# Low parts of the weights last in each split product; the convolution of x ahead of the attention's gate in the first layer

## The chip, the cores and the metric

The kernel runs on one core of one Trainium2 chip. The metric is device time in microseconds (us), from one launch that holds the whole computation. A core has five engines that each work through a queue of their own in order: TensorE (PE, with its weight loads, PEld), VectorE (DVE), ScalarE (ACT), GpSimd (POOL) and SyncE (SP, which here only issues transfers). They wait for one another through semaphores; transfers (DMA) run beside them.

## The reference, cut to what matters

Two layers over 512 tokens of x and 256 tokens of a context, with 1024 channels. Each layer has a trunk (normalization, one input projection, three token mixers that gates merge, an output projection) and a feed-forward part of 16,384 one-neuron experts, of which each of 8 heads picks 16 for a token.

```python
for l in range(2):
    p = modulate(rms_norm(h)) @ w_in[l]                  # 1024 -> q, k, v, pool, conv (3 x), gates (3 x)
    attn = attn_out_norm(diff_attn(q, [k, kc], [v, vc])) # kc, vc: from the context's projection
    pool = pool_branch(p_pool, pool_w[l])
    conv = (b_gate * depthwise_conv(c_gate * p_conv)) @ conv_out_w[l]
    g = sigmoid(p_gates)
    h = h + mod * ((g0 * attn + g1 * pool + g2 * conv) @ w_out[l])
    # experts, in chunks of 128 tokens
    q = (xn2 @ w_q).reshape(T, 8, 2, 128)
    s1, i1 = top_k(q[:, :, 0] @ keys1, 16); s2, i2 = top_k(q[:, :, 1] @ keys2, 16)
    top_s, pos = top_k(s1[:, None] + s2, 16); eidx = (i1 * 128 + i2)[pos]
    hid = gelu(xn2 . u_emb[eidx]);  w = softmax(top_s) * hid
    h = h + mod * sum(w * v_emb[eidx])
    # the context hc goes the same way in the first layer (in the last only its k and v are made)
```

All is in float32.

## The kernel before, in words

**Split products.** Every large product is made of operands that are split into a high part (rounded to TensorE's format) and a low part (the rest): `split` (line 92) copies the high part on ScalarE and subtracts it on VectorE, for weights as for activations. `mm3` (lines 96 to 100) then issues three matmuls for each of the 8 slices of the contracted dimension, all into one bank of the accumulation memory: high by high, high by low, low by high. In `proj_t`, `hidden` and `values` the weight is the left operand, so the third matmul of every slice reads the low part of the weight: `wlo` in a projection, `ul` in the experts' first product, `vl` in their second.

**Weights.** `load_w` (line 136) fetches a projection's weight as two halves of four slices on SyncE's queue into `wraw` (three buffers) and splits each into `whi` and `wlo` (three buffers each). `proj_t` (line 153) makes a group of 24 matmuls for a 128-row block of the result.

**Mixers.** `mixers` (line 980) goes through a string of letters: p pooling, c convolution, g attention's gate with the norm of its heads, k the convolution's gates made ahead, o merge and output projection. Over x in the first layer the string is "gco" with three banks for the results (line 972). Just before stand the norm and the top-16 picks of the context's feed-forward part (`ctx_ffn`).

**Experts.** The context (256 tokens) in the first layer and the first 128 tokens of x in the second are done row by row: `gathered` (line 848) has GpSimd fetch for every one of the 128 picks of 128 tokens a row of `peer_u` or `peer_v` by index into a ring of three `row` buffers (line 855); VectorE multiplies and sums it (lines 868 and 878). There are 768 fetches. Their priority is 40000 behind their place in the program, so they are spread under later work. All other tokens (512 of x in the first layer, 384 in the second) go through all experts densely: `gates` (line 750 on) builds with one-hots `gA`, `gE`, `gB` on VectorE and small matmuls `gps` a table of gate weights `G`; `hidden` (line 767) makes gelu(u y) in tiles of 128 experts, `uh` and `ul` in two buffers each; `weigh` (line 796) multiplies it with `G` and splits the product into `wh` and `wl`; `values` (line 820) multiplies with the experts' second weights, blocks of 8 tiles, `vh` and `vl`, in four banks `dps`. In the second layer 20 of 32 chunks of hidden products are stored first; for the other 12, `experts` (line 1123) goes through hidden and values in turn, with EC + 2 = 4 buffers for `vh` and `vl`.

**What sets the order.** The code gives every instruction a priority by its place in the program, shifted in places by `prio`; a scheduler with a simulated time line then writes out one fixed order for every engine, in which buffers and data allow it. On the chip each engine works strictly in that order.

**Stages in the trace (us).** To 360 modulation, norm and q, k, v of the first layer; to 850 attention, the context's mixers and pooling; to 1360 the context's keys and the mixers over x; 1380 to 2290 keys, gates and hidden products; to 3000 values; to 3790 the second layer's trunk; to 4400 its keys, gates and stored hidden products; 4415 to 4730 hidden and values in turn; to the end the rest of the values. Fetches of rows run from 997 to 2874 and from 3800 on.

## Time and profile before

| | |
|---|---|
| median of 3 runs | 5121.54 us (5118.99 to 5127.41) |
| profiled execution | 5126.48 us |
| its span, from first to last instruction | 5124.7 us |
| mean granted clock of TensorE | 0.975 |
| TensorE busy | 4846.5 us, 95% |
| its weight loads busy | 4187.1 us, 82% |
| VectorE busy | 3946.3 us, 77% |
| ScalarE busy | 1984.5 us, 39% |
| GpSimd busy | 1199.9 us, 23% |

The busy time of TensorE counts the whole of each matmul, with ends that are modelled, so a busy TensorE can still be slower than at its pace. The list of waits puts each idle time of an engine down to the work that ended it, as engine, tile, line <- engine, tile, line. A window gives the busy time of each engine within a stretch, and the clock granted there as a share of full speed.

### The profile page before, as it was taken

Reading aid. Unit: us, or ns where it says so; the run is one execution under the profiler, and the core shown is the slowest. Engines: PE = TensorE matmul, PEld = TensorE weight load, DVE = VectorE, ACT = ScalarE, POOL = GpSimd, SP = SyncE. Lnnn points to the kernel's source line nnn. Section 1 sums busy time; section 2 is a strip of 40 time slices with the busy share of each in tenths; the row PEclk is TensorE's granted clock in tenths of the full one; section 3 lists DMA queues with packets and bytes.
Section 4 is the critical chain, followed back from the end, with each engine's and each line's share of the span. In section 5 each row is a group of like instructions: output and inputs, shape, how many; then the busy total and the mean of one; then the engine's idle time right before and its main releaser. Section 6 shows DMA issues by size and latency. Waiting matters only on the chain.

```text
span 5124.7 us, 74008 instructions
## 1 busy us (share of the span) xinstructions
PE 4846.5 (95%) x27373; PEld 4187.1 (82%) x27373; DVE 3946.3 (77%) x7996; ACT 1984.5 (39%) x2970; POOL 1199.9 (23%) x1060
## 2 busy tenths in 40 slices
PE   8999999798799999989999999999999999899999
PEld 5689787576588788768888879888679889899999
DVE  5468785977799998568888766777459999787885
ACT  4346665222233344323222334555334344332333
POOL 0012000144433343243334100100000433244320
PEclk9999999899899999999999999999899999999999
DMA  8668554488888888999999734543355888988995
GB/s 308 239 201 237 179 169 129 145 271 276 281 302 270 297 300 323 323 315 320 342 335 337 261 114 161 175 135 118 120 169 173 282 297 329 319 313 292 335 330 177
DMA packets 509419, 1280.77 MB, mean 250 GB/s; under 512 B 42880, under 2 KB 225024, under 8 KB 500736
## 3 DMA queue, kind: packets, MB, share of 16 engines
q1 hardware_dynamic: 302816, 669.35, 38.7%
q0 software_dynamic: 132352, 449.90, 26.1%
q10 hardware_dynamic: 73888, 156.79, 8.2%
q8 instruction: 215, 3.52, 0.3%
q14 instruction: 148, 1.21, 0.1%
HBM read 1098.13 MB, written 177.73 MB: 249 GB/s over the span
## 4 chain that ended last, share of the span: by engine, by line
PE 47%; DMA 14%; issue 11%; DVE 9%; POOL 3%; ACT 1%; POOLq 0%; DVEq 0%; ACTq 0%; SPq 0%
DMA row<-peer_v,ix 8%; PE dps L100 6%; PE dps L99 6%; PE dps L98 6%; DMA row<-peer_u,ix 5%; PE mm L98 4%; PE mm L100 4%; PE mm L99 4%; PE hid L100 4%; PE hid L98 4%; PE hid L99 3%; POOL row L855 3%; DVE gacc L878 2%; PE gps L760 1%; PE qk L100 1%
## 5 line engine op out<-in xcount | busy, mean ns | idle before, releaser
L100 PE MATMUL hid<-yh,ul 128*128 128x512 f32 (+1 forms) x2048 | 760.8, 373 | 55.3 <-DVE ul L94 54.9
L855 POOL DMA_INDIRECT row<-peer_v,ix x384 | 586.7, 1528 | 876.9 <-DVE gacc L878 537.4
L98 PE MATMUL hid<-yh,uh 128*128 128x512 f32 (+1 forms) x2048 | 758.3, 371 | 21.0 <-ACT yh L286 13.1
L855 POOL DMA_INDIRECT row<-peer_u,ix x384 | 503.5, 1311 | 1113.7 <-DVE row L868 614.3
L99 PE MATMUL hid<-yl,uh 128*128 128x512 f32 (+1 forms) x2048 | 755.9, 369 | 3.6 <-DVE yl L287 3.6
L100 PE MATMUL dps<-wh,vl 128*128 128x512 f32 (+1 forms) x2048 | 740.9, 364 | 11.8 <-DVE vl L94 11.8
L99 PE MATMUL dps<-wl,vh 128*128 128x512 f32 (+1 forms) x2048 | 741.1, 364 | 7.0 <-DVE wl L94 7.0
L98 PE MATMUL dps<-wh,vh 128*128 128x512 f32 (+1 forms) x2048 | 735.3, 364 | 8.9 <-ACT vh L93 8.9
L98 PE MATMUL mm<-hi,whi 128*128 128x512 f32 (+1 forms) x1856 | 665.5, 359 | 19.6 <-ACT rg L481 6.0
L100 PE MATMUL mm<-hi,wlo 128*128 128x512 f32 (+1 forms) x1856 | 658.6, 357 | 25.3 <-DVE wlo L94 25.0
L99 PE MATMUL mm<-lo,whi 128*128 128x512 f32 (+1 forms) x1856 | 659.8, 356 | 1.7 <-DVE lo L94 1.7
L878 DVE SCALAR_TENSOR_TENSOR gacc<-row,gw,gacc 128x1024 f32<-128x1024 f32 x381 | 488.2, 1281 | 166.9 <-DMA row<-peer_v,ix 165.4
L868 DVE SCALAR_TENSOR_TENSOR row<-row,gx 128x1024 f32<-128x1024 f32 x384 | 466.9, 1222 | 168.5 <-DMA row<-peer_u,ix 167.9
L94 DVE TENSOR_TENSOR wlo<-wraw,whi 128x1024 fp32r<-128x1024 f32 (+1 forms) x356 | 428.1, 1204 | 178.5 <-ACT whi L93 175.7
L93 ACT ACTIVATE uh<-uraw 128x1024 fp32r<-128x1024 f32 x256 | 271.3, 1060 | 689.5 <-PE hid L99 657.4
L93 ACT ACTIVATE whi<-wraw 128x1024 fp32r<-128x1024 f32 (+1 forms) x356 | 369.9, 1043 | 385.3 <-PE mm L99 270.1
L93 ACT ACTIVATE vh<-vraw 128x1024 fp32r<-128x1024 f32 x256 | 270.1, 1057 | 633.6 <-PE dps L99 387.9
L100 PEld LDWEIGHTS hid<-yh,ul 128*128 128x128 f32 x2048 | 391.2, 191 | 107.4 <-DVE ul L94 69.3
L98 PEld LDWEIGHTS hid<-yh,uh 128*128 128x128 f32 x2048 | 392.1, 192 | 63.6 <-ACT yh L286 14.7
L100 PEld LDWEIGHTS dps<-wh,vl 128*128 128x128 f32 x2048 | 386.3, 189 | 53.2 <-DVE vl L94 12.7
L99 PEld LDWEIGHTS hid<-yl,uh 128*128 128x128 f32 x2048 | 391.4, 191 | 44.7 <-DVE yl L287 5.0
L98 PEld LDWEIGHTS dps<-wh,vh 128*128 128x128 f32 x2048 | 386.6, 189 | 49.9 <-ACT vh L93 9.7
(337 smaller groups left out, 9481.1 us busy)
## 6 DMA issues: line engine op xcount, KB each, us to landing
uraw<-uT SPq DMA_DIRECT2D x256, 512.0 KB
vraw<-v SPq DMA_DIRECT2D x256, 512.0 KB
wraw<-w_in SPq DMA_DIRECT2D x216, 512.0 KB
gd<-gst ACTq DMA_DIRECT2D x28, 2048.0 KB
mw<-w_mod SPq DMA_DIRECT2D x96, 512.0 KB
wraw<-wq SPq DMA_DIRECT2D x80, 512.0 KB
hidd<-ge ACTq DMA_DIRECT2D x128, 256.0 KB
G<-gd SPq DMA_DIRECT2D x32, 1024.0 KB
```

Of the source, the lines that this page charges most:

```text
L93: self.nc.scalar.activation(hi, src, AF.Copy)
L94: self.nc.vector.tensor_tensor(lo, src, hi.bitcast(F32), op=OP.subtract)
L98: mm(ps, lh, rh, start=start, stop=False)
L99: mm(ps, lh, rl, start=False, stop=False)
L100: mm(ps, ll, rh, start=False, stop=stop)
L760: nc.tensor.matmul(ps[:, t], A[:, a_, :, t_], B[x][:, a_, :, t_], start=x == 0, stop=x == 1)
L855: nc.gpsimd.indirect_dma_start(out=r, out_offset=None, in_=a[t], in_offset=bass.IndirectOffsetOnAxis(ap=idx[:, s:s + 1], axis=0))
L868: nc.vector.scalar_tensor_tensor(out=r, in0=r, scalar=1.0, in1=x, op0=OP.mult, op1=OP.mult, accum_out=hid[:, k:k + 1])
L878: nc.vector.scalar_tensor_tensor(acc, r, w[:, k:k + 1], acc, op0=OP.mult, op1=OP.add)
```

## The change

`mm3` takes all slices of a group at once. It issues two matmuls for each slice first, and only then the third of every slice. With `late` 0 these last ones are those that read the low part of the left operand, with 1 those of the right operand; each call picks the one that is the weight. The number of matmuls stays the same. `uh` and `ul` get three buffers for two. In the turns of the second layer `vh` and `vl` get three for four. In the mixers over x in the first layer the convolution comes ahead of the attention's gate ("cgo"), the results have six banks for three, and the second half of every weight gets buffers from a pool of its own, `wmore`, three each beside the three there were. The numbers of the lines behind shift by 1 to 5.

```diff
-    def mm3(self, ps, lh, ll, rh, rl, start, stop):
+    def mm3(self, ps, terms, late, start=True, stop=True):
         mm = self.nc.tensor.matmul
-        mm(ps, lh, rh, start=start, stop=False)
-        mm(ps, lh, rl, start=False, stop=False)
-        mm(ps, ll, rh, start=False, stop=stop)
+        for i, (lh, ll, rh, rl) in enumerate(terms):
+            mm(ps, lh, rh, start=start and i == 0, stop=False)
+            mm(ps, *((lh, rl), (ll, rh))[late], start=False, stop=False)
+        for i, (lh, ll, rh, rl) in enumerate(terms):
+            mm(ps, *((ll, rh), (lh, rl))[late], start=False, stop=stop and i == len(terms) - 1)
...
     def load_w(self, src, kts, cols):
...
-            h = self.wpool.tile([P, step, cols], F32R, tag="whi", name="whi", bufs=self.wbufs)
-            lw = self.wpool.tile([P, step, cols], F32R, tag="wlo", name="wlo", bufs=self.wbufs)
+            pool, n = (self.wmore, 3) if k0 and self.wmore else (self.wpool, self.wbufs)
+            h = pool.tile([P, step, cols], F32R, tag="whi", name="whi", bufs=n)
+            lw = pool.tile([P, step, cols], F32R, tag="wlo", name="wlo", bufs=n)
...
     def proj_t(self, pp, w, streams, kts=KT, tag="mm"):
...
-            for k in range(kts):
-                self.mm3(ps, w[0][k], w[1][k], s.h[:, k], s.l[:, k], k == 0, k == kts - 1)
+            self.mm3(ps, [(w[0][k], w[1][k], s.h[:, k], s.l[:, k]) for k in range(kts)], 0)
...
     def hidden(self, l, y, up, uq, cs, ahead, keep=False):
...
-                    uh = up.tile([P, KT, P], F32R, name="uh", bufs=2)
-                    ul = up.tile([P, KT, P], F32R, name="ul", bufs=2)
+                    uh = up.tile([P, KT, P], F32R, name="uh", bufs=3)
+                    ul = up.tile([P, KT, P], F32R, name="ul", bufs=3)
...
-                for k in range(KT):
-                    self.mm3(hid, uh[:, k], ul[:, k], y.h[:, k], y.l[:, k], k == 0, k == KT - 1)
+                self.mm3(hid, [(uh[:, k], ul[:, k], y.h[:, k], y.l[:, k]) for k in range(KT)], 0)
...
     def values(self, l, n, cs, W, pools, vq, acc, first, last=None):
...
-                for e in range(4 * EC):
-                    self.mm3(ps, V[e][0][:, db * P:(db + 1) * P], V[e][1][:, db * P:(db + 1) * P], W[0][e], W[1][e],
-                             e == 0, e == 4 * EC - 1)
+                b = slice(db * P, (db + 1) * P)
+                self.mm3(ps, [(V[e][0][:, b], V[e][1][:, b], W[0][e], W[1][e]) for e in range(4 * EC)], 0)
...
-        self.EC, self.stored = 2, 20
+        self.EC, self.stored, self.wmore = 2, 20, None
...
                 with ExitStack() as e2:
-                    hm = self.mixers(l, X, self.pool(e2, f"fl{l}", 3, PSUM), xp, "gco")
+                    self.wmore = self.pool(e2, f"wx{l}")
+                    hm = self.mixers(l, X, self.pool(e2, f"fl{l}", 6, PSUM), xp, "cgo")
+                self.wmore = None
...
-                        self.values(l, n, cs, self.weigh(l, n, va, cs, had), lambda dq: (vb, 3, vb, EC + 2), vq, acc, c == S + EC)
+                        self.values(l, n, cs, self.weigh(l, n, va, cs, had), lambda dq: (vb, 3, vb, EC + 1), vq, acc, c == S + EC)
```

On TensorE, inside one tile of hidden products in the second layer (`hid` is the result, `yh` and `yl` the parts of the tokens, `uh` and `ul` of the weight), before, two slices and the start of the third:

```order
L98 MATMUL hid<-yh,uh 128x384
L99 MATMUL hid<-yl,uh 128x384
L100 MATMUL hid<-yh,ul 128x384
L98 MATMUL hid<-yh,uh 128x384
L99 MATMUL hid<-yl,uh 128x384
L100 MATMUL hid<-yh,ul 128x384
L98 MATMUL hid<-yh,uh 128x384
```

and now, the last three slices of a tile and the beginning of the next tile:

```order
L101 MATMUL hid<-yh,uh 128x384
L102 MATMUL hid<-yl,uh 128x384
L101 MATMUL hid<-yh,uh 128x384
L102 MATMUL hid<-yl,uh 128x384
L101 MATMUL hid<-yh,uh 128x384
L102 MATMUL hid<-yl,uh 128x384
L104 MATMUL hid<-yh,ul 128x384 x8
L101 MATMUL hid<-yh,uh 128x384
```

The eight matmuls that read `ul`, one in each slice before, stand together behind the sixteen that read `uh`.

On TensorE, around the norm of the context ahead of its keys in the first layer (`nps` is the sum of squares, `ntr` the transposes; `po` is the context attention's or x's attention output, `mm` a projection), before:

```order
L100 MATMUL mm<-hi,wlo 128x512
L275 MATMUL nps<-nsq,ones 128x256 x2
L293 MATMUL ntr<-ident,nfull 128x128 x10
L98 MATMUL mm<-hi,whi 128x512
L99 MATMUL mm<-lo,whi 128x512
```

and now:

```order
L456 MATMUL tr_6337<-ident,at 128x128 x4
L101 MATMUL po<-th,hv_6152 128x512
L102 MATMUL po<-th,hv_6153 128x512
L104 MATMUL po<-tl,hv_6152 128x512
L280 MATMUL nps<-nsq,ones 128x256 x8
L298 MATMUL ntr<-ident,nfull 128x128 x16
L101 MATMUL mm<-hi,whi 128x256
L102 MATMUL mm<-lo,whi 128x256
```

The projections of the attention's gate (`mm` with 512 columns) that stood between the parts of the norm have left; the norm's matmuls stand together between the last attention product and the first key projection (256 columns).

On VectorE, at the end of the second layer's gates (`gA`, `gE`, `gB` one-hots of the gates; `gacc` and `row,ghid` fetched rows; `ul` the splits of hidden weights), before:

```order
L878 SCALAR_TENSOR_TENSOR gacc<-row,gw,gacc 128x1024
L94 TENSOR_TENSOR ul<-uraw,uh 128x1024
L750 TENSOR_TENSOR gA<-iota_38404,sl_35870 128x1024
L752 TENSOR_TENSOR gB_40098<-gE,sl_35872 128x1024
L753 TENSOR_TENSOR gB_40099<-gE,sl_35873 128x1024
L878 SCALAR_TENSOR_TENSOR gacc<-row,gw,gacc 128x1024
L94 TENSOR_TENSOR ul<-uraw,uh 128x1024
L878 SCALAR_TENSOR_TENSOR gacc<-row,gw,gacc 128x1024 x3
L94 TENSOR_TENSOR ul<-uraw,uh 128x1024
L868 SCALAR_TENSOR_TENSOR row,ghid<-row,gx 128x1024 x2
L94 TENSOR_TENSOR ul<-uraw,uh 128x1024 x2
```

and now:

```order
L879 SCALAR_TENSOR_TENSOR gacc<-row,gw,gacc 128x1024
L754 TENSOR_TENSOR gE<-iota_38408,sl_35875 128x1024
L755 TENSOR_TENSOR gB_40074<-gE,sl_35876 128x1024
L756 TENSOR_TENSOR gB_40075<-gE,sl_35877 128x1024
L753 TENSOR_TENSOR gA<-iota_38408,sl_35874 128x1024
L755 TENSOR_TENSOR gB_40102<-gE,sl_35876 128x1024
L756 TENSOR_TENSOR gB_40103<-gE,sl_35877 128x1024
L879 SCALAR_TENSOR_TENSOR gacc<-row,gw,gacc 128x1024
L869 SCALAR_TENSOR_TENSOR row,ghid<-row,gx 128x1024 x6
L811 TENSOR_TENSOR ge<-ge,G 128x384 x4
L94 TENSOR_TENSOR wl<-ge,wh 128x384 x3
```

The splits `ul` that stood between and behind the last gate instructions have moved ahead of them; behind the last gate come six fetched rows and then at once the product of hidden and gate (`ge<-ge,G`, line 809 before, 811 now).

## Rows read from the trace of the kernel before

**Rows 1.** The page's busy table: engine, busy us, share of the span, instructions.

```profile
PE 4846.5 (95%) x27373; PEld 4187.1 (82%) x27373; DVE 3946.3 (77%) x7996; ACT 1984.5 (39%) x2970; POOL 1199.9 (23%) x1060
```

**Rows 2.** TensorE's waits, whole span: us in total, times, longest us.

```profile
PE hid L100 <- DVE ul L94: 54.9, 33, 5.8
PE mm L100 <- DVE wlo L94: 28.9, 16, 4.2
...
PE dps L100 <- DVE vl L94: 11.8, 2, 11.0
...
PE dps L98 <- ACT vh L93: 8.9, 2, 7.1
```

**Rows 3.** Windows: stretch, length, busy us by engine, granted clock, DMA share, GB/s.

```profile
1060.00:1340.00 280.00, 242.72 (x996) 191.77 (x994) 203.78 (x252) 67.17 (x83) 121.25 (x107) 0.96 0.82 274
1380.00:2290.00 910.00, 880.67 (x4974) 736.30 (x4973) 770.77 (x1704) 322.75 (x484) 330.35 (x231) 0.99 0.87 303
2434.00:2562.00 128.00, 128.00 (x567) 106.01 (x566) 110.61 (x148) 36.23 (x46) 46.33 (x36) 1.00 0.97 341
3960.00:4388.00 428.00, 402.86 (x2787) 384.39 (x2786) 396.38 (x828) 175.28 (x283) 159.27 (x99) 0.98 0.83 300
4415.00:4730.00 315.00, 295.37 (x1647) 291.70 (x1648) 248.77 (x336) 104.24 (x149) 125.58 (x91) 0.97 0.88 304
```

**Rows 4.** Waits of TensorE, then VectorE, in 1060 to 1340.

```profile
PE mm L100 <- DVE wlo L94: 21.9, 12, 4.2
...
DVE row L868 <- DMA row<-peer_u,ix: 30.2, 17, 3.9
```

**Rows 5.** Lines in 1060 to 1340: count, busy us, mean ns, idle before.

```profile
L878 DVE SCALAR_TENSOR_TENSOR gacc<-row,gw,gacc 128x1024 f32<-128x1024 f32 x49 | 62.9, 1283 | 38.4 <-DMA row<-peer_v,ix 38.2
...
L868 DVE SCALAR_TENSOR_TENSOR row<-row,gx 128x1024 f32<-128x1024 f32 x48 | 58.3, 1222 | 30.2 <-DMA row<-peer_u,ix 30.2
...
L94 DVE TENSOR_TENSOR wlo<-wraw,whi 128x1024 fp32r<-128x1024 f32 x41 | 50.0, 1219 | 0.0
...
L585 DVE SCALAR_TENSOR_TENSOR y<-z,cols,y 128x512 f32<-128x512 f32 x6 | 4.5, 753 | 0.2
...
L600 ACT ACT_TABLE_LOAD x2 | 2.6, 1283 | 0.0
```

**Rows 6.** Timeline of TensorE from 848 to 890: start, us, instruction.

```profile
848.61 0.39 PE L98 MATMUL mm<-hi,whi 128*128 128x512 f32 x1
...
888.77 0.39 PE L98 MATMUL mm<-hi,whi 128*128 128x256 f32 x1
```

**Rows 7.** TensorE's waits in 1380-2290, 2290-3000, 3790-4415 and (three) 4415-4730.

```profile
PE hid L100 <- DVE ul L94: 16.8, 12, 4.0
...
PE dps L100 <- DVE vl L94: 11.0, 1, 11.0
...
PE hid L100 <- DVE ul L94: 24.4, 13, 5.8
...
PE hid L100 <- DVE ul L94: 13.7, 8, 5.0
PE dps L98 <- ACT vh L93: 7.1, 1, 7.1
PE dps L100 <- DVE vl L94: 0.7, 1, 0.7
```

**Rows 8.** VectorE's waits in 3960 to 4388.

```profile
DVE row L868 <- DMA row<-peer_u,ix: 14.3, 8, 4.6
DVE gacc L878 <- DMA row<-peer_v,ix: 11.6, 7, 5.5
DVE ul L94 <- ACT uh L93: 2.4, 4, 0.9
```

**Rows 9.** Timeline of ScalarE's queue, then VectorE, in 4380 to 4420.

```profile
4389.27 0.33 ACTq L763 DMA_DIRECT2D gd<-gst  x1
...
4415.14 1.96 DVE L809 TENSOR_TENSOR ge<-ge,G 128x384 f32<-128x384 f32 x4
```

More of the change, by code (lines that the diff above doesn't have):

```diff
@@ L315, in qkv @@
                             for t in range(2):
-                                for k in range(KT):
-                                    xh, xl = s.sub(k, 2 * u + t)
-                                    self.mm3(ps[:, t], xh, xl, w[0][k], w[1][k], k == 0, k == KT - 1)
+                                self.mm3(ps[:, t], [(*s.sub(k, 2 * u + t), w[0][k], w[1][k]) for k in range(KT)], 1)
                             if kind == "v":
@@ L456, in head @@
             self.split(th, tl, tr)
-            self.mm3(po, v[0][:, kt], v[1][:, kt], th, tl, kt == 0, kt == nk - 1)
+            self.mm3(po, [(v[0][:, kt], v[1][:, kt], th, tl)], 1, kt == 0, kt == nk - 1)
         ot = ap_.tile([P, nq * P], F32, tag="ot", name="ot", bufs=2)
@@ L777, in hidden @@
                     nc.sync.dma_start(raw.rearrange("p k e -> p (k e)"), a["uT"][l, 4 * c + e])
-                    uh = up.tile([P, KT, P], F32R, name="uh", bufs=2)
-                    ul = up.tile([P, KT, P], F32R, name="ul", bufs=2)
+                    uh = up.tile([P, KT, P], F32R, name="uh", bufs=3)
+                    ul = up.tile([P, KT, P], F32R, name="ul", bufs=3)
                     self.split(uh, ul, raw)
                 hid = uq.tile([P, y.n], F32, name="hid", bufs=3)
-                for k in range(KT):
-                    self.mm3(hid, uh[:, k], ul[:, k], y.h[:, k], y.l[:, k], k == 0, k == KT - 1)
+                self.mm3(hid, [(uh[:, k], ul[:, k], y.h[:, k], y.l[:, k]) for k in range(KT)], 0)
                 with self.prio(-ahead):
```

## The prediction, made before the changed kernel had run

> **What bounds the kernel now.** I read the page's busy table first. TensorE (PE) is busy for 4846.5 of 5124.7 us, which looks like no room; its weight loads and VectorE (DVE) stand well below [rows 1]. A busy PE is not a PE at its pace, so I took the pace from a stretch without holes: 567 matmuls of 512 columns in 128.0 us at clock 1.00, 0.226 us each [rows 3]. Next the list of PE's waits: the four that the change aims at are weights' low parts made by DVE, `ul` 54.9, `wlo` 28.9, `vl` 11.8 us, and a smaller one for a high part, `vh` 8.9 [rows 2]. Together 104.5 us, 2% of the time.
>
> Then I asked which engine keeps PE waiting in each stretch. In the first layer's mixers over x, 996 matmuls would take 225 us of the 280 there [rows 3]: 55 us are lost, and 21.9 of them is the wait for `wlo` [rows 4]. DVE is busy for 203.8 us of the same 280, and sits another 68.4 us (38.2 + 30.2) in front of a gathered row that has not landed [rows 3, 5]. It works in the order written, so 272 of 280 us are spoken for: splits stand behind late rows. 97 rows (49 + 48) pass there [rows 5], one every 2.89 us, though DVE needs only 1.25 for one; the ring of three `row` buffers (line 855) goes round no faster.
>
> **What the change does not touch.** PE carries 28,735 rows in its queue before and after; no matmul is added. ScalarE gets 11 more table loads of 1.283 us [rows 5], 14 us in all on an engine at 39%; I price them at nothing, and at 14 us if all stood on the path.
>
> **Term 1: first layer, mixers over x, -22 us.** In the old order 96 matmuls of the gates (21.7 us at 0.226) stand between and around the context's norm, from 848.61 until the first key projection at 888.77 [rows 6]; in the new one the norm's matmuls stand alone and nothing covers its chain. The 40.2 us shrink to no less than 18.5; I take 22, so the keys start 18 us earlier, and the 96 matmuls are issued later instead. Behind the keys the convolution runs where the old order had the gate's norm; its first three weights are split before DVE's long top-16 work, six groups of 24, 33 us of matmuls. But six more `wlo` and about ten smaller instructions of the convolution now stand ahead of the first fetched row on DVE: 6 x 1.219 plus 10 x 0.75 [rows 5] is 14.8 us, less some 5 for the eleven short instructions of the norm that leave this place (bounded by 0 and 11 x 0.75). So fetching starts 18 - 10 = 8 us earlier. From there DVE's order has 112 fetches before the last tile of the output projection, where it had 117: 5 x 2.89 is 14 us. 8 + 14 = 22. If fetches set the end, the extra `wlo` buffers and six banks give no more. Ends: +5 if the bare norm and the gate's norm chain, now among fetches at 2.89 us each, cost what is saved; -45 if PE alone sets the end (the 55 lost less 10).
>
> **Term 2: first layer, hidden products, -18.** PE waits 16.8 us there for `ul` [rows 7], and the clock is at 0.99 over 910 us [rows 3], some 9 us of work lost. Low parts are now needed 16 matmuls (3.6 us) later and three buffers let a split start a whole tile (24 matmuls, 5.4 us) earlier; the longest of all such waits was 5.8 [rows 2]. I take 14 of the waits and 4 of the clock. Ends: -26 and -4 (DVE, busy 770.8 of 910 [rows 3], hands the delay on).
>
> **Term 3: first values, -7.** The one wait of 11.0 us for `vl` [rows 7] falls behind 32 matmuls with high parts (four groups of eight), 7.2 us. Ends -9 and 0.
>
> **Term 4: handover of the products' right sides, 0.** `wh` of a block is now read until the last eight matmuls of its last group, so the next block's splits have 9 to 16 matmuls where they had over 20. Four groups are interleaved there, eight matmuls per part (1.8 us), against some 0.75 us of DVE (128x512 [rows 5]). About 30 handovers at up to 0.4 us: 0 to +12.
>
> **Term 5: second layer until the first values, 0.** PE waits 24.4 us for `ul` [rows 7], and I give back none of it. DVE is busy 396.4 of 428 us and waits 25.9 (14.3 + 11.6) for rows [rows 3, 8]: it is the bound. The new order runs PE's hidden tiles ahead of the gates, until their buffers are full, and leaves the last five gate rounds alone on DVE; the last gate has 226 splits `ul` in front of it instead of 219 and 303 of the fetches' second kind instead of 300. 7 x 1.219 plus 3 x 1.283 [rows 5] is 12.4 us more DVE work, against 2.4 us of DVE's waits for `uh` [rows 8], and I take 10 of the row waits, as fetches now stand evenly, one per four gate instructions. From the last gates' write to the first product of hidden and gate lie 25.9 us (4389.27 to 4415.14) [rows 9], which the old order fills with four hidden tiles and the new one leaves empty; those tiles were done before. What remains behind that point is the same, so the end moves only as the last gate moves. Ends -12 and +12.
>
> By occupancy the row says DVE 396.4 against weight loads 384.4 of 428. The Trainium skill (Perfetto Trace Analysis, Identifying the Most-Contended Engine) says to improve the engine with the highest occupancy, judging TensorE by its weight loads. This change takes no instruction off DVE; by that rule term 5 is 0, as I have it, and term 2, where DVE also leads (770.8 to 736.3), would fall to -4 and the sum to -47.
>
> **Term 6: second layer, rest, -10.** `ul` 13.7 and `vh` 7.1 [rows 7] go, 20.8. In the loop that mixes hidden and values, `vh` and `vl` have three buffers instead of four: the second tile of each of 24 quarter blocks waits until the tile before is read, 24 matmuls (4.3 us at 295.37 / 1647 = 0.179 [rows 3]) for two splits (2 x 1.22 = 2.4 [rows 5]). I charge 0.5 us for each of 22, 11. Ends -22 and +20.
>
> **Term 7: elsewhere, -4** (28.9 - 21.9 = 7.0 of `wlo` [rows 2, 4]); ends -7 and 0.
>
> Sum: -22 - 18 - 7 + 0 + 0 - 10 - 4 = -61. The profiled execution took 5126.5 us (span 5124.7 and 1.8 around it), so 5065.5; the median run, 5121.5, lies 5 lower, so 5060.5. I predict 5060.
>
> **Rivals.** *All of it comes out*: the four waits and nothing given back, 5121.5 - 104.5 = 5017. For it: the waits are short (33 of `ul`, the longest 5.8) and a whole tile of lead covers them; against it: 272 of 280 us of DVE in term 1, and term 5.
> *Handed on*: DVE's queue, fetches and splits in one order, is the bound almost everywhere, and PE waits at another place. Then only term 3 is left: 5114. For it: the late rows [rows 4, 8]; against: in 1380 to 2290 DVE has 139 us free.
> *Slower*: three buffers in the mixed loop. Place: second `vl` of each quarter block, behind late rows on DVE. At 4 us per block, about one late row (the row waits of the first layer ran to 3.9 [rows 4]), it costs 24 x 4 = 96 instead of 11, and the sum becomes +24: 5146. It decides from 61 / 24 = 2.5 us per block above my 0.5. Against it: PE's waits for `vl` there are 0.7 us now, in all [rows 7].
>
> **Chances.** Forecast 0.62, all of it 0.15, handed on 0.13, slower 0.10. A difference under 0.2% (10 us, below 5111 or above 5132) can't be told from none. Half of "handed on" lies beyond it: faster 0.62 + 0.15 + 0.06 = 0.83, same 0.07, slower 0.10. The forecast's own range is 5030 to 5090 (terms 1 and 6 at half of their ends). For 8 in 10 I leave out the slow rival and the upper part of "handed on", and keep "all of it" but for its lowest part: 5012 to 5112.
>
> **What would show it.** In the changed profile: PE's waits for `ul` and `vl` under 10 us in all (terms 2, 3, 6); rows still at about 2.9 us apart in the first layer's mixers, with its last output tile about 22 us earlier (term 1); an idle PE for 25 to 45 us ahead of the second layer's first values, with the last gate at most 12 us later counted from the stage's start (term 5); waits for `vl` below 0.5 us per quarter block (term 6). Rows that come faster than 2.9 us apart, or PE idle in the mixed loop, would make it wrong.

## The result, and the profile after

The change made the kernel slower: 5190.14 us (median of 4 runs, 5187.74 to 5197.82) against 5122.34 before; ratio 1.0134, 95% interval [1.0117, 1.0152]. The forecast was 5060 with a range of 5012 to 5112. The profiled execution took 5197.82 us, its span 5196.1, 71.4 more than before.

The busy table hardly differs from [rows 1]; ScalarE has 11 instructions more:

```profile
PE 4866.2 (94%) x27373; PEld 4202.6 (81%) x27373; DVE 3936.6 (76%) x7996; ACT 2018.2 (39%) x2981; POOL 1234.9 (24%) x1060
```

TensorE's waits over the whole span (us, times, longest), which answer to [rows 2]:

```profile
PE dps L102 <- DVE wl L94: 29.3, 20, 4.2
PE dps L101 <- ACT vh L93: 28.7, 4, 24.8
PE nps L280 <- ACT nsq L279: 24.6, 9, 12.1
PE dps L101 <- ACT wh L93: 23.2, 10, 14.3
PE hrb L505 <- ACT hrh L93: 22.1, 2, 17.4
PE sc L437 <- ACT p L444: 18.5, 16, 2.3
PE hss L495 <- ACT osq L494: 15.6, 2, 14.0
...
PE dps L104 <- DVE vl L94: 13.7, 5, 7.3
PE gps L763 <- ACT gst L765: 12.4, 8, 4.7
...
PE mm L104 <- DVE wlo L94: 3.0, 1, 3.0
```

Four of these waits before, which [rows 2] leave out:

```profile
PE hrb L502 <- ACT hrh L93: 13.9, 2, 9.2
...
PE nps L275 <- ACT nsq L274: 9.5, 6, 5.2
...
PE hss L492 <- ACT osq L491: 7.0, 2, 6.8
PE dps L99 <- DVE wl L94: 7.0, 5, 3.4
```

`ul` is gone from the list and `wlo` has shrunk from 28.9 to 3.0. Which edit took them away the list does not say; the experiments do, and for `wlo` it is not the late order. In their place stand `wl`, `vh` and `wh`, the operands of the second expert product, `p`, the attention's exponentials, and ScalarE's steps in the norms (`nsq` for the norm of all channels, `osq` and `hrh` for the norm of attention's heads). The list got no shorter, so I went to a table by stage: the time of one first or last matmul of a tile in TensorE's timeline, in each profiled execution. (`rsc` are the scores of the context's keys, `hid` and `dps` the two expert products; 0 and 1 are the layers.)

| us | before | after | difference | gained or lost in the stage |
|---|---|---|---|---|
| first `rsc` (end of the attention stage and the context's norm) | 900.6 | 933.1 | +32.5 | +32.5 |
| first `hid`, 0 (end of the mixers over x) | 1361.8 | 1390.1 | +28.3 | -4.2 |
| first `dps`, 0 (end of hidden) | 2286.2 | 2310.7 | +24.5 | -3.8 |
| last `dps`, 0 (end of values) | 3006.2 | 3064.3 | +58.1 | +33.6 |
| first `hid`, 1 (end of the trunk) | 3803.8 | 3857.2 | +53.4 | -4.7 |
| first `dps`, 1 | 4420.1 | 4463.0 | +42.9 | -10.5 |
| last `hid`, 1 (end of the mixed loop) | 4722.0 | 4749.5 | +27.5 | -15.4 |
| last `dps`, 1 | 5120.3 | 5191.7 | +71.4 | +43.9 |

Three rows lose 110 us: the first and the two runs of values alone. (Of the last two rows 42 matmuls, some 7 us, only changed sides: 2312 matmuls stand behind the last `hid` for 2270.)

The first row has three parts. The last matmul of q, k and v ends 10.4 us later (376.8 for 366.4). The last attention product ends 47.3 us later (896.1 for 848.8), so the attention stage, with 2976 matmuls in both kernels, loses 36.9. From there to the first `rsc`, where the gate's projections stood before, 14.8 us are won. The loss ahead of the attention is not chance: q, k and v end at 366 to 368 us in the ten kernels here that make them slice by slice, and at 374 to 378 in the eight with the late order. Up to there TensorE has the same 2408 matmuls and next to no waits; the cause was not looked for.

The stages that lose in windows (columns as in [rows 3]), before:

```profile
366.00:848.00 482.00, 452.51 (x2977) 404.01 (x2976) 384.22 (x818) 307.09 (x521) 53.27 (x139) 0.99 0.61 183
2286.00:3006.00 720.00, 702.33 (x3081) 578.28 (x3080) 575.88 (x770) 203.65 (x258) 220.77 (x158) 0.99 0.88 304
4722.00:5120.00 398.00, 394.64 (x2271) 394.03 (x2270) 315.34 (x464) 135.66 (x182) 85.59 (x66) 1.00 0.82 286
```

and after, with the stretch in the mixers over x that answers to the first of [rows 3] as the second row:

```profile
377.00:895.00 518.00, 474.34 (x2974) 422.22 (x2975) 382.30 (x818) 323.48 (x534) 53.26 (x140) 0.93 0.58 173
1075.00:1355.00 280.00, 241.00 (x1004) 189.96 (x1003) 209.70 (x270) 73.99 (x94) 122.66 (x109) 0.92 0.84 288
2311.00:3065.00 754.00, 713.37 (x3082) 581.93 (x3081) 585.79 (x779) 201.01 (x258) 226.20 (x167) 0.98 0.87 297
4750.00:5192.00 442.00, 417.96 (x2312) 408.62 (x2310) 323.32 (x474) 135.00 (x184) 88.17 (x68) 0.97 0.79 263
```

The same matmuls take 518 us for 482 and 754 for 720. The granted clock fell with them, from 0.99 to 0.93 in the attention stage and from 1.00 to 0.97 at the end. In the attention stage TensorE's idle time makes some 14 of the 36 us (43.7 for 29.5); the other 22 are busy time of as many matmuls, at the lower clock (474.3 for 452.5). (Single executions of kernels that agree in a stage can differ there by 10 us and more: the second layer's trunk, by the table's marks, took 791 to 807 us in the six kernels with sigmoids and the old projections there. A difference of that size in a single pair of executions shows nothing.)

In that stretch of the mixers the fetched rows answer to [rows 5] like this:

```profile
L879 DVE SCALAR_TENSOR_TENSOR gacc<-row,gw,gacc 128x1024 f32<-128x1024 f32 x47 | 60.2, 1281 | 24.5 <-DMA row<-peer_v,ix 24.1
...
L869 DVE SCALAR_TENSOR_TENSOR row<-row,gx 128x1024 f32<-128x1024 f32 x47 | 57.3, 1221 | 40.1 <-DMA row<-peer_u,ix 39.9
```

47 + 47 = 94 rows in 280 us, 2.98 us each: the ring goes round no faster than before, as forecast.

**Values.** One handover between blocks at the end of the second layer (start, length, instruction, idle before). ScalarE:

```profile
5119.41 1.06 ACT L93 ACTIVATE vh<-vraw 128x1024 fp32r<-128x1024 f32 x1 [0.32 <-PE dps L102]
5120.37 3.40 ACT L93 ACTIVATE wh<-gel 128x384 fp32r<-128x384 f32 x8
```

VectorE:

```profile
5120.16 1.23 DVE L94 TENSOR_TENSOR vl<-vraw,vh 128x1024 fp32r<-128x1024 f32 x1 [2.96 <-PE dps L104]
5121.30 0.55 DVE L841 TENSOR_TENSOR acc<-dps,acc 128x384 f32<-128x384 f32 x1
5121.77 1.22 DVE L94 TENSOR_TENSOR vl<-vraw,vh 128x1024 fp32r<-128x1024 f32 x1
5122.90 1.95 DVE L94 TENSOR_TENSOR wl<-gel,wh 128x384 fp32r<-128x384 f32 x4
```

TensorE:

```profile
5119.21 1.55 PE L104 MATMUL dps<-wh,vl 128*128 128x384 f32 x8
5120.94 0.81 PE L101 MATMUL dps<-wh,vh 128*128 128x384 f32 x3 [0.17 <-ACT wh L93]
5121.90 0.44 PE L101 MATMUL dps<-wh,vh 128*128 128x384 f32 x1 [0.16 <-DVE acc L841]
5123.51 0.44 PE L102 MATMUL dps<-wl,vh 128*128 128x384 f32 x1 [1.16 <-DVE wl L94]
```

And ScalarE at a handover before:

```profile
5050.51 1.57 ACT L93 ACTIVATE wh<-gel 128x384 fp32r<-128x384 f32 x3 [3.79 <-PE dps L100]
5051.98 1.04 ACT L93 ACTIVATE vh<-vraw 128x1024 fp32r<-128x1024 f32 x1
5052.93 1.75 ACT L93 ACTIVATE wh<-gel 128x384 fp32r<-128x384 f32 x4
```

In the changed kernel, at 5119.21, the eight matmuls with `vl` begin; they are the last readers of all eight `wh`. ScalarE then splits the next eight `wh` in one go, 3.40 us. VectorE stands behind the end of the block: the sum `acc`, a split `vl`, and only at 5122.90 the first `wl`, for which TensorE waits until 5123.51. From the end of the eight at 5120.76 to there pass 2.75 us with four matmuls in them. Before, each `wh` came free three matmuls after the one ahead of it; the first three were split at 5050.51 and the next four from 5052.93, while TensorE went on without a wait.

**Attention stage.** ScalarE's table loads there, by the line of the function that needs them (exponential, then the three gates' sigmoids), before:

```profile
L441 ACT ACT_TABLE_LOAD x21 | 26.9, 1283 | 1.6 <-DVE mx L438 1.3
...
L551 ACT ACT_TABLE_LOAD x11 | 14.1, 1283 | 0.6 <-ACT ot L459 0.4
...
L481 ACT ACT_TABLE_LOAD x6 | 7.7, 1283 | 4.9 <-PE mm L100 4.8
...
L600 ACT ACT_TABLE_LOAD x4 | 5.1, 1283 | 0.1
```

and after:

```profile
L444 ACT ACT_TABLE_LOAD x27 | 34.6, 1283 | 6.8 <-DVE mx L441 6.0 <-ACT ot L462 0.4
...
L554 ACT ACT_TABLE_LOAD x13 | 16.7, 1283 | 0.2
L484 ACT ACT_TABLE_LOAD x8 | 10.3, 1283 | 5.9 <-PE mm L104 5.4 <-ACT ot L462 0.4
...
L603 ACT ACT_TABLE_LOAD x6 | 7.7, 1283 | 0.1
```

54 instead of 42. The page has 11 more in all (120 for 109), so what was added stands in this one stage, on the engine that TensorE waits for there; its largest wait in the stage, before and after:

```profile
PE sc L434 <- ACT p L441: 8.2, 7, 2.2
```

```profile
PE sc L437 <- ACT p L444: 18.3, 15, 2.3
```

### The profile page after: what moved, and what is told of

The parts are those of the page before. It is cut to its first block, busy times and chain, and to the rows that moved or that the text cites. A ratio compares the mean times of both kernels' runs of the same rounds, so it can differ in the third digit from the quotient of the medians.

```text
span 5196.1 us, 73979 instructions
## 1 busy us (share of the span) xinstructions
PE 4866.2 (94%) x27373; PEld 4202.6 (81%) x27373; DVE 3936.6 (76%) x7996; ACT 2018.2 (39%) x2981; POOL 1234.9 (24%) x1060
## 4 chain that ended last, share of the span: by engine, by line
PE 55%; DMA 16%; issue 12%; DVE 10%; POOL 4%; ACT 3%; SPq 0%; ACTq 0%; POOLq 0%; DVEq 0%
DMA row<-peer_v,ix 8%; PE mm L101 6%; PE mm L102 6%; PE mm L104 6%; DMA row<-peer_u,ix 4%; PE dps L102 4%; PE dps L104 4%; POOL row L856 4%; PE dps L101 4%; PE hid L104 3%; PE hid L102 3%; PE hid L101 3%; PE qk L101 2%; PE qk L102 2%; PE qk L104 2%
## 5 line engine op out<-in xcount | busy, mean ns | idle before, releaser
L856 POOL DMA_INDIRECT row<-peer_v,ix x384 | 602.7, 1570 | 861.8 <-DVE gacc L879 491.2
L102 PE MATMUL dps<-wl,vh 128*128 128x512 f32 (+1 forms) x2048 | 751.5, 370 | 29.4 <-DVE wl L94 29.3
L856 POOL DMA_INDIRECT row<-peer_u,ix x384 | 522.7, 1361 | 1054.1 <-DVE row L869 608.0
L101 PE MATMUL mm<-hi,whi 128*128 128x512 f32 (+1 forms) x1856 | 648.8, 362 | 16.4 <-ACT hi L93 8.4
L102 PE MATMUL mm<-lo,whi 128*128 128x512 f32 (+1 forms) x1856 | 645.4, 360 | 0.0
L104 PE MATMUL hid<-yh,ul 128*128 128x512 f32 (+1 forms) x2048 | 472.2, 367 | 0.0
L104 PE MATMUL dps<-wh,vl 128*128 128x512 f32 (+1 forms) x2048 | 459.0, 363 | 13.7 <-DVE vl L94 13.7
L102 PEld LDWEIGHTS dps<-wl,vh 128*128 128x128 f32 x2048 | 393.2, 192 | 78.8 <-DVE wl L94 37.9
L101 PEld LDWEIGHTS mm<-hi,whi 128*128 128x128 f32 x1856 | 365.1, 197 | 70.1 <-ACT hi L93 9.0
L104 PEld LDWEIGHTS dps<-wh,vl 128*128 128x128 f32 x2048 | 372.3, 188 | 55.5 <-DVE vl L94 15.3
```

Of the source, the lines that this page charges most:

```text
L101: mm(ps, lh, rh, start=start and i == 0, stop=False)
L102: mm(ps, *((lh, rl), (ll, rh))[late], start=False, stop=False)
L104: mm(ps, *((ll, rh), (lh, rl))[late], start=False, stop=stop and i == len(terms) - 1)
L856: nc.gpsimd.indirect_dma_start(out=r, out_offset=None, in_=a[t], in_offset=bass.IndirectOffsetOnAxis(ap=idx[:, s:s + 1], axis=0))
```

## The experiments

In the diffs `mm3o` is the old `mm3`, slice by slice. "Old" means that order. Each ratio is against the kernel before, with its interval; stages are from each kernel's own profile. In the series that these runs belong to, the kernel before has medians from 5121.6 to 5128.1 us, so the difference of two medians from different series is uncertain by some 6 us.

**Values old.**

```diff
-                self.mm3(ps, [(V[e][0][:, b], V[e][1][:, b], W[0][e], W[1][e]) for e in range(4 * EC)], 0)
+                for e in range(4 * EC):
+                    self.mm3o(ps, V[e][0][:, b], V[e][1][:, b], W[0][e], W[1][e], e == 0, e == 4 * EC - 1)
```

> The changed kernel, but values (both layers) issues its three matmuls slice by slice as before. Theory A (handover): with the low parts of the weight last, all eight wh of a block are read until the last eight matmuls of its last group, and the next block's splits of wh and wl run late; that is the 2 to 8 us which most blocks of values lost. Expected: blocks of the first layer back to 43.5 us each and the stage to about 720 us (754 in the changed kernel), the last ten blocks of the second layer back to 33.3 us and about 400 us (444), total about 5190 - 70 = 5120 (5105 to 5135). Rival B (the loss comes from ahead: VectorE is behind with late fetched rows, whatever the order of the products): blocks stay at 45 to 51 and 35 to 37 us, total above 5170.

Measured: 5134.12 us, ratio 1.0014 [0.9999, 1.003]. The two stages in windows:

```profile
2309.00:3029.00 720.00, 702.52 (x3083) 578.05 (x3083) 588.72 (x782) 203.87 (x259) 230.52 (x167) 0.99 0.89 311
4727.00:5140.00 413.00, 403.82 (x2314) 401.43 (x2312) 320.63 (x471) 138.09 (x184) 88.32 (x65) 1.00 0.80 278
```

720 us as before, and 413 (with the 42 more matmuls of the change, and some 7 us above the kernel before without them). The order in values costs 56 us by the medians, 61 by the ratios and 64 in the two stages; its place is shown.

**Values with `wl` last instead of `vl`.**

```diff
-... for e in range(4 * EC)], 0)
+... for e in range(4 * EC)], 1)
```

> The changed kernel, but in values the two matmuls with wh of each slice stand first and the eight with wl last. By theory A wh of a block is free during its last group's first pass and wl during the second, 24 matmuls before the next block reads each again: blocks at 43.5 and 33.3 us, total 5110 to 5130, with the 11 us wait for vl at the first block back. A third reading E (standing the third matmuls together is itself slow, by weight loads or banks) has the blocks as slow as in the changed kernel, total 5180 to 5200.

Measured: 5185.94, ratio 1.0112 [1.009, 1.0134]: as slow as the change, and my reading of the handover failed here. TensorE's waits in the first layer's values:

```profile
PE dps L102 <- DVE vl L94: 23.0, 7, 19.3
PE dps L104 <- DVE wl L94: 10.6, 8, 2.5
```

With `wl` last, `wh` comes free early, but TensorE waits for `wl` again, at eight places, and for `vl`, which is now needed at once. That the eight `wl` are the ones that pass in a row would explain the first; it was not tested apart. By its number this is what reading E expected. The next experiment speaks against E in the first layer.

**More buffers for `wh`, order as changed** (in the first layer alone).

```diff
-                wh = va.tile([P, n], F32R, name="wh", bufs=4 * self.EC + (0 if l else 1))
+                wh = va.tile([P, n], F32R, name="wh", bufs=4 * self.EC + (0 if l else 5))
```

> The changed kernel with 13 buffers for wh instead of 9 in the first layer's values; the order of the matmuls stays as changed. By the handover theory five of the eight next high parts can then be split before the block of before gives any back: the stage falls from 754 us to 720 to 735 and the total by about 25, to 5165 (5155 to 5175). Rival (VectorE's series of wl splits and its fetched rows set it, whatever wh does): stage at 745 to 755, total 5185 to 5195.

Measured: 5164.79, ratio 1.0075 [1.0055, 1.0095], within 1 us of the expected number. The stage and its waits:

```profile
2304.00:3032.00 728.00, 703.89 (x3082) 578.58 (x3082) 585.35 (x782) 206.04 (x260) 223.15 (x167) 0.99 0.88 308
```

```profile
PE dps L101 <- ACT wh L93: 16.1, 1, 16.1
PE dps L102 <- DVE wl L94: 5.9, 5, 1.9
```

728 us for 754, with the order untouched: in the first layer the handover of the right sides is the cause, not the order as such. TensorE is busy for 703.89 us, where it was 702.33 before and 713.37 with the change, so third matmuls that stand together are not slow in themselves (reading E). In the second layer this was not tried; there only the order was undone, and E is not excluded. What is left for `wh` is one wait of 16.1 us at the first block, where before `vl` was waited for, 11.0 [rows 7].

**Projections, q, k, v and the attention's product old.**

```diff
+            for k in range(kts):
+                self.mm3o(ps, w[0][k], w[1][k], s.h[:, k], s.l[:, k], k == 0, k == kts - 1)
...
+            self.mm3o(po, v[0][:, kt], v[1][:, kt], th, tl, kt == 0, kt == nk - 1)
```

> The changed kernel, but projections, q, k, v and the attention's product with v issue slice by slice as before; hidden, values, the order of the mixers over x and the buffers stay changed. Theory C: the new order of the projections' matmuls moves the attention's scores and transposes against the projections of the first layer's attention stage, which grew from 482 to 519 us with 58 us more at the low clock. Expected: that stage back to 480 to 490 us, total about 5190 - 40 = 5150. Rival D (it is the convolution ahead of the gate, whose weights are asked for at the end of the attention): the stage stays at 510 to 520 us and the total at 5180 to 5195.

Measured: 5155.68, ratio 1.0051 [1.0031, 1.007]. The total is as theory C has it. The stage by the expected measure fell to 498 only, 16 above the kernel before; the first `rsc` comes at 901.4, against 933.1 with the change and 900.6 before, with the 15 us in it that the new order of the mixers wins behind the stage.

**The mixers over x undone.**

```diff
-                    self.wmore = self.pool(e2, f"wx{l}")
-                    hm = self.mixers(l, X, self.pool(e2, f"fl{l}", 6, PSUM), xp, "cgo")
+                    hm = self.mixers(l, X, self.pool(e2, f"fl{l}", 3, PSUM), xp, "gco")
```

> The changed kernel, but the mixers over x in the first layer in the order gate, convolution, output with three banks and no further weight buffers, as before. By theory C the attention stage stays long (510 to 520 us), and the mixers over x lose the 20 us they gained against the end of the attention (47 us behind the kernel before at its end, 28 behind at the first hidden product): total about 5190 + 20 = 5210. By rival D the attention stage falls to 480 to 490 and the total to about 5170.

Measured: 5178.47, ratio 1.0092 [1.007, 1.0114]: faster by 12 (by the ratios 21), where C had expected slower by 20. The first `rsc` comes at 938.4 and the first `hid` at 1392.6, 2.5 us later than with the change. The attention's last product ends at 884.6, 11.5 us ahead of the change and still 35.8 behind the kernel before. So the convolution ahead of the gate makes at most a smaller part of the loss up to there, and inside the whole change it gains next to nothing. The waits for `wlo` are back, though every product has the late order:

```profile
PE mm L104 <- DVE wlo L94: 24.2, 15, 2.3
```

What took them away is therefore the edit of the mixers (its order, banks and weight buffers were not tried apart): with it they are at most 4.6 us in every trace, without it 17.4 to 28.9, whichever order the products have. The waits for `nsq`, `hrh` and `osq` go the other way: 52 to 62 us in all with it, 30 to 34 without.

**Projections alone old** (q, k, v and the attention's product stay changed): the first two added lines above.

> The changed kernel with the projections alone slice by slice as before (q, k, v and the attention's product stay changed). Theory C, narrowed: the projections of the context's mixers, which share the attention stage, set its order. Then the first score of the context's keys comes at 900 to 910 us (933 in the changed kernel, 901 with all three undone) and the total is 5155 to 5165. Rival: q, k, v or the attention's product does it; then 920 us or later, and 5170 to 5190.

Measured: 5162.93, ratio 1.0066 [1.004, 1.0093]; first `rsc` at 905.4, both as expected.

**Only the projections of the attention stage old**: a flag set ahead of the first layer's `attend` and cleared ahead of `ctx_ffn`.

```diff
+            if self.early:
+                for k in range(kts):
+                    self.mm3o(ps, w[0][k], w[1][k], s.h[:, k], s.l[:, k], k == 0, k == kts - 1)
```

> The changed kernel, but the projections of the first layer's attention stage alone (the context's mixers and the pooling of x) slice by slice as before; all other projections, q, k, v and the attention's product stay changed. Theory C, narrowed once more: these alone set the order of that stage. The first score of the context's keys then comes at 900 to 912 us (933 in the changed kernel, 907 with all projections undone), the second layer's trunk keeps its 556 to 560 us (565 to 571 in every kernel with old projections), and the total is 5150 to 5162. Rival: the split of the order elsewhere matters too; 920 us or later, 5170 or more.

Measured: 5177.53, ratio 1.0092 [1.0065, 1.0119], with runs from 5160 to 5186. The first `rsc` comes at 905.1: these projections alone set the stage. The total missed: the keys and mixers behind it took 468 us for 457 in the change, and I did not find why. The table loads go with the stage. In the eleven kernels with sigmoids whose first `rsc` comes at 894 to 911, 46 to 49 loads stand ahead of it; in the five where it comes at 928 to 938, 60 or 61.

**No change of ScalarE's table between attention and gates**, in the changed kernel and in the kernel before.

```diff
-                    nc.scalar.activation(g, ..., AF.Sigmoid)
+                    nc.scalar.activation(g, ..., AF.Exp)
```

> The changed kernel with the exponential in place of the sigmoid in the three kinds of gates (another function is computed there), which ScalarE does without a change of table between gates and attention: 40 table loads instead of 120, the order of all other instructions exactly as in the changed kernel. Read against the same edit of the kernel before. Theory T (the 12 further table loads in the attention stage, on the engine that TensorE waits for there, and the drops of the clock that follow): the first score of the context's keys comes within 10 us of the kernel before with the same edit, where the two differ by 32.5 now, and the two totals differ by 68 - 25 = 40 to 50. Rival O (the order of the matmuls itself): they differ by 25 or more at that point, and by 60 or more in all.

> The kernel before with the exponential in place of the sigmoid in the gates: 39 table loads instead of 109, order as before. By theory T it gains less than the changed kernel with the same edit does, by some 25 us: about 10 to 25 us faster than before. By rival O both gain the same.

Measured: 5155.55 (1.0069 [1.0046, 1.0093]) and 5097.93 (0.9957 [0.9946, 0.9969]). All other instructions stand in the order they had, and two table loads are left in the stage in either kernel. The first `rsc` comes at 898.6 and 892.5: 6.1 us apart, where it was 32.5. Theory T holds at that place: some 26 of the 32 us go with the table changes, where the twelve further loads themselves are 15.4 us; that waits and the clock behind them are the rest is argued, not shown apart. The 10 us of q, k and v stay (378.4 for 367.8). In all the two kernels differ by 57.6, between T's 40 to 50 and O's 60: only ten less than the 68 of the pair with sigmoids. In these traces the hidden products lose 11 of what the stage saves (+7.3 us in this pair, -3.8 in the other).

**What is left with all of that undone** (values, projections and attention old; of the change stay hidden, its buffers and the mixers), and the same without the mixers.

> The changed kernel with values, projections, q, k, v and the attention's product all slice by slice as before; what stays of the change is the late order in hidden, three buffers for uh and ul, three for vh and vl, and the mixers over x. If the two losses found (values 56 us, projections 34) are independent, the total is about 5190 - 56 - 34 = 5100 (5090 to 5115), faster than before by 20 to 30. Rival (they share a cause, such as one late engine or the clock): 5125 or more.

> As the kernel with values, projections and attention slice by slice, and also with the mixers over x in the order gate, convolution, output, three banks and no further weight buffers. If the order of the mixers is worth the 2 to 3 us that the traces show up to the first hidden product, the total lies within 8 us of that kernel, about 5100; if it is worth the 22 us of the prediction's first term, about 5120.

Measured: 5118.5, ratio 0.9992 [0.9981, 1.0003], and 5115.27, 0.9988 [0.9977, 0.9998]. Both are where the kernel before is; the 20 to 30 us that I expected to be left over are not there. The forecast's other gains are not hidden behind the two losses: in the total they did not come. With the mixers the first `hid` comes 14.8 us earlier (1351.2 for 1366.0), and the hidden products behind it take 931.1 us for 915.2.

**The late order in hidden, with the old buffers and with the new** (both with the late order in the projections behind the attention stage, everything else as before), and without it.

```diff
-                    uh = up.tile([P, KT, P], F32R, name="uh", bufs=2)
-                    ul = up.tile([P, KT, P], F32R, name="ul", bufs=2)
+                    uh = up.tile([P, KT, P], F32R, name="uh", bufs=3)
+                    ul = up.tile([P, KT, P], F32R, name="ul", bufs=3)
...
-                        ... lambda dq: (vb, 3, vb, EC + 2), vq, acc, c == S + EC)
+                        ... lambda dq: (vb, 3, vb, EC + 1), vq, acc, c == S + EC)
```

> The kernel before with the late order in two places only: the hidden products, and the projections behind the first layer's attention stage (its keys and mixers over x, the second layer's trunk). All buffers and the order of the mixers as before (two for uh and ul, four for vh and vl). If the waits for ul (54.9 us) are handed on to the gates and to the right sides of the mixed loop, as in the other kernels, the total is 5122 less about 15: 5100 to 5112. If they are gained, 5070 to 5085. Theory F on the vh wait of 25 us ahead of the second layer's first block: it comes from three buffers for vh and vl; then it is 7 again here. Rival G: it comes from hidden tiles that run ahead of the last gates; then 20 to 27 here too.

> As the kernel with the late order in hidden and in the projections behind the attention stage, but with three buffers for uh and ul and three for vh and vl, as in the change. By theory F the first block of the second layer waits 20 to 27 us for vh and the mixed loop 7 to 10 for vl, and the total lies about 10 us above that kernel; by rival G the totals agree within 5 us.

> The kernel before with the late order only in the projections behind the first layer's attention stage; hidden and everything else as before. The second layer's trunk falls from 565 to about 558 us, the first layer's keys and mixers by 2 to 5: total about 5122 - 10 = 5112 (5104 to 5118).

Measured: 5109.7 (0.9969 [0.9955, 0.9983]), 5114.35 (0.9981 [0.9967, 0.9995]) and, without the late order in hidden, 5103.66 (0.9953 [0.9936, 0.997]). The order that the waits for `ul` called for gains nothing in hidden; the intervals do not tell whether it loses the 6 us. Over the whole span TensorE waits 23.0 us for `ul` with the late order and the old buffers, and not at all with the new. Waits in the mixed loop, in the same order:

```profile
PE dps L108 <- ACT vh L93: 22.7, 1, 22.7
PE hid L104 <- DVE ul L94: 11.5, 6, 3.1
```

```profile
PE dps L108 <- ACT vh L93: 24.8, 1, 24.8
PE dps L110 <- DVE vl L94: 10.3, 3, 6.5
```

The wait ahead of the first block (7.1 before [rows 7]) is there with four buffers too, so theory F falls. Rival G holds in part: without the late order in hidden the wait is 14.9 us already. Three buffers bring 10 us of waits for `vl` in place of 11.5 for `ul` here: one wait for another.

**The mixers over x alone** (the kernel before with this edit), and together with the late order of the projections behind the attention stage.

```diff
-                    hm = self.mixers(l, X, self.pool(e2, f"fl{l}", 3, PSUM), xp, "gco")
+                    self.wmore = self.pool(e2, f"wx{l}")
+                    hm = self.mixers(l, X, self.pool(e2, f"fl{l}", 6, PSUM), xp, "cgo")
```

> The kernel before with the mixers over x in the new order alone, six banks and the further weight buffers; all products slice by slice, all other buffers as before. By the prediction's first term the first hidden product of the first layer comes 22 us earlier (1340 for 1362) and the total is 5100. By what the pairs with and without this part showed, it comes 0 to 10 us earlier, and the five fetches left for later give that back in the hidden products: total within 8 us of the kernel before.

> The kernel before with two parts of the change: the mixers over x in the new order with six banks and further weight buffers, and the late order in the projections behind the first layer's attention stage. If their gains of 17 and 18 to 24 us add up: 5122 - 35 to 40 = 5082 to 5090. If the late order makes the new order of the mixers worthless, as inside the whole change, where undoing it gained 12 us: 5100 to 5110.

Measured: 5105.56 (0.9973 [0.9956, 0.999]) and 5085.1 (0.9921 [0.9904, 0.9938]). Alone, the new order of the mixers brings the first `hid` to 1350.0, 11.8 us earlier (in the fastest of its ten executions), and the total down by 17; I had expected 0 to 10, and 8 at most. The two parts add up in the total (17 and 24 alone, 42.5 together), and this kernel is 0.8% faster than the one before. They do not add up at the place: with both, the first `hid` comes at 1362.8, as late as before, and the trace is ahead only from the hidden products on (912.4 us for 924.4 there, 708.9 for 720.0 in the values behind).

## Why the prediction was wrong, point by point

- **The attention stage was in no term.** Its one trace in the working is the sentence on ScalarE's "11 more table loads", priced "at nothing, and at 14 us if all stood on the path". The number was right, the place was not looked up, and an engine busy for 39% of the span is busy for 64% of that stage (307.09 of 482 us). Measured: 32.5 us at the first `rsc`, 36.9 in the stage itself; some 26 go when the table changes go, and 10 of the 68 us in the total. The 10.4 us that q, k and v lose ahead of it were in no term either. The Trainium skill (ScalarE: Activation LUTs, What ACT_TABLE_LOAD costs) prices a switch at 2.66 us, with a drain beside the load; the trace shows 1.283 for the load and no such drain around it (medians of 0.02 us ahead and 0.01 behind), so the loss above the 15 us of loads is not in the loads themselves.
- **Term 4, the handover of `wh` and `wl`: 0, with an end of +12.** This is the step that decided. I had the mechanism ("the next block's splits have 9 to 16 matmuls where they had over 20") and sized it by TensorE's distance against one split of VectorE at a time. What queues at that moment was left out: ScalarE gets all eight `wh` free at once and needs 3.40 us for them, and on VectorE the sum `acc` and a `vl` stand ahead of the first `wl`, which cannot begin before its `wh`. Undoing it gains 56 us; the trace shows 33.6 in the first layer and some 36 in the last stage. In the first layer four more buffers for `wh` give 26 of the 34 back with the order untouched.
- **Term 3, first `vl`: -7.** The wait passed to `wh`, 14.3 us in the first block of the changed kernel. Gain: none.
- **Terms 2, 5 and 6 (hidden): -18, 0, -10.** The waits for `ul` went, as forecast, and came back elsewhere: as waits of the gates' products (`gps`, 23.7 us for 1.3) and for the first `vh`, 24.8 us. That is the rival "handed on", which had 0.13. The stages won 3.8, 10.5 and some 8 in the one trace (15.4 less what changed sides), but the late order in hidden gains nothing in the total: 5109.7 and 5114.35 with it, 5103.66 without. The rule of the Trainium skill that was weighed beside term 5 (Perfetto Trace Analysis, Identifying the Most-Contended Engine) had put term 2 at -4; the trace shows -3.8, which does not tell it from nothing. Term 5 (0, with -12 to +12) came out at -10.5, and the empty stretch ahead of the first values is there, as the order had shown. The slower rival, three buffers in the mixed loop, was wrong in size: 9.1 us of waits for `vl`, not 96.
- **Term 1: -22.** Nearly right from where its working starts: from the last attention product to the first `hid` pass 494.0 us in the changed kernel and 491.5 with the mixers alone, for 513.0 before. What it held fixed is the start: with the mixers alone the attention's end comes 9.7 us later (858.5 for 848.8), inside the change 11.5 (896.1 for 884.6 without this part). Its worse end, the bare norm and the chain of the gate's norm, is what TensorE now waits for in place of `wlo` (`nsq`, `hrh` and `osq`, 62.3 us for 30.4). In the total it gains 17 alone and nothing beside the change in hidden (5118.5 with it, 5115.27 without), and inside the whole change undoing it made the kernel faster by 12. Why is not settled; the whole order of all engines is drawn up anew for every edit, and the runs show the result, not the reason.
- **The sum of four waits, 104.5 us, was taken as something to win.** With the parts tried in turn, the parts that gain are the mixers (17) and the late order of the projections behind the attention stage (24: 5103.66 against 5127.66 of the same series). In its trace the second takes 11.5 us off the waits for `wlo` (17.4 for 28.9; what is left stands in the mixers over x), so where its other 12 come from is open. The waits for `ul`, twice as long as those for `wlo`, brought nothing.
- **What the change does not touch.** The traces have 27373 matmuls in both kernels, as forecast; the number 28,735 in the working stands in none.

## What to carry to other kernels

A list of waits names who came last, not what is short. Nor does a wait that is gone name the edit that took it: here that for `wlo` in the mixers went with the edit of the mixers and not with the order of the products. Before pricing an order that puts one operand's use last, find every other operand that is now held until the end of the group, and write down, engine by engine, what stands in the queue between its release and its next use. Where a change moves instructions of an engine that looks idle, look at its busy share in the stage where they land and not over the span, and count the changes of ScalarE's table between functions as instructions of their own. A change of many parts is best taken apart on the chip: here two of the parts gain 0.8%, and the others cost more than that.

## What was not expected of the hardware

Replacing the sigmoid by the exponential, which computes another result, makes the kernel before faster by 24 us with 70 table loads fewer (89.8 us of ScalarE's time at 1.283), on an engine that the span shows as 39% busy. And a lower clock went with more waits of TensorE: in the attention stage it was idle for 44 us of 518 in place of 29 of 482, and the mean granted clock of 0.93 in place of 0.99 is some 72 us at the lower of its two levels (1.2 of 2.4 GHz) in place of some 10. Idle time in sum does not order the clock, though: without the table changes the stage has 24 us idle of 483 at 0.96 and 21 of 474 at 0.98.
